# Sums through HBM moved apart, a normalisation moved forward and block products reordered, in a one-core hybrid backbone

## The chip, the core and the metric

The kernel runs on one core of a Trainium2 chip. The metric is device time in microseconds from launch to the last store; smaller is better. TensorE (PE) does the matmuls, VectorE (DVE), ScalarE (ACT) and GpSimd (POOL) the rest, and SyncE (SP) issues most transfers. POOL issues the transfers that add into their destination, ACT a few stores.

## The reference

Two layers on 1024 latent tokens of width 1024, with 256 context tokens, in float32. The change lies in layer 0.

```python
def conformer_conv(va, vg, p):
    u = va * jax.nn.sigmoid(vg)
    u = depthwise_conv(u, p["conv_w"], p["conv_b"], CONV_PAD)   # 31 taps
    return jax.nn.silu(layernorm(u, p["ln_g"], p["ln_b"]))

def rglru_branch(xb, p, h0, with_outputs):
    u = depthwise_conv(xb, p["sconv_w"], p["sconv_b"], SHORT_CONV_PAD)
    u2 = jnp.stack([u, u[:, ::-1]], axis=2)
    a, bx = lru_coeffs(u2, p)            # sigmoid gates, exp, sqrt
    hT, hs = lru_scan(a, bx, h0, with_outputs)
    ...
    y = hs[:, :, 0] + hs[::-1, :, 1]

def even_mixer(h, h0, p):
    z = h @ p["w_in"]
    va, vg, ga, xb, gb = jnp.split(z, ...)
    y_a = conformer_conv(va, vg, p) * jax.nn.silu(ga)
    y_b, hT = rglru_branch(xb, p, h0, True)
    y_b = y_b * jax.nn.silu(gb)
    return jnp.concatenate([y_a, y_b], axis=-1) @ p["w_out"], hT
```

Layer 1 is a pooling mixer with a grouped product (folded into its input weights ahead of time) and an output product; a last RMS norm follows.

## The kernel before

Every array stands transposed: 128 channels on the partitions, 1024 tokens along a row, so a 1024-wide array is eight tiles (`KT = 8`) with two halves of 512 tokens (`HALF`). A float32 factor is split into a high part in the reduced format and the low remainder, and every product is three matmuls: high x high, high x low, low x high. ACT makes the high part (`cast`), DVE or POOL the low one. `mm3_fixed` is one 128-row output half: 8 x 3 matmuls of 512 columns.

Order. The tile framework orders instructions by a simulated timeline, but through most of layer 0 the order is written out by hand: `on(engine, ...)` ties each instruction behind the one before it on its engine, and `act`, `cast`, `gp`, `vec` go through it while `fixed[0]` is true. Each engine runs its list in order, so an instruction that waits holds up all behind it. Where `fixed[0]` is false, the framework places ACT, DVE and POOL instructions; block products of `ga` stay tied on PE. Plain transfers on SP are placed by the framework; those of `sum_copies` are held behind the last weight load (`latest[0]`). `plus` (line 818) is a transfer on POOL's queue that adds its source into its destination, in POOL's written order.

**The rounds (loop over `j`, eight turns; turn `j` is round `j`).** Turn `j` computes `vg`, the recurrence branch input `xb` of the next channel tile, the gates and `va`, makes `u = va * sigmoid(vg)`, and carries the recurrence of the turn before (`state`). On ACT it runs in this order: two tanh (`rec_tanh`, one per direction), the cast of the `va` weights, a sigmoid, the cast `uh`, later exp and sqrt. On DVE `rec_scan` runs once per direction; then `rec_sum` adds the two directions and stores the sum to `yb_raw[j]` in HBM. The tiles rotate: the two tanh of a turn overwrite the backward tile (first) and the forward tile (second) that were scanned at the end of the turn before. `fill(n)` puts n steps of the 31-tap `conv` (one DVE instruction of 512 columns or so) at a place in DVE's order; `conv(j)` turns `us[j]` into its convolution, `ln_sums` adds it up for the norm.

**Sums through HBM.** The product for `ga` is later done by a seven-product block scheme (Strassen-Winograd) on halves of weights, channels and tokens. It needs sums of blocks, and those are made in HBM while the rounds run: `sum_copies(j)` issues the plain copies of turn `j`, `sum_adds(j)` the adding transfers. `h_raw` is the input, high plus low; `neg` two negated halves of it (tiles `n`); `h_ops["t1"]` to `["t4"]` the sums of inputs, `wsums` those of weights.

**After the rounds.** `gb` products, then `wob`: the product of `y_b` with half of the output weights, eight tiles `m` of two halves. `wob_evict` scales a half on ACT, adds `x` on POOL and stores it. Between these, DVE finishes the conv; `mean_parts`, `ln_mean`, `ln_square`, `ln_add`, `ln_root`, `ln_scale`, `ln_silu` are the layer norm of `us`, half by half, with row means by a product with ones (banks `mu` and `ms_ln`; the scale factors `lnr` stay in the banks `c1` and one half of `xb` until `ln_scale` has read them).

**Block products.** For each column `q` (0 to 3) products 1 to 7 of 12 matmuls go into banks `a`, `c`, `b`; `ga_op(n)` splits the n-th weight block in `GORDER`, `ga_raw` loads two of them. After product 1, ACT copies `a` into `b` (line 1645 for q > 0). `ga_silu`, `ga_gate` multiply `us` by the gates, `ga_sum` and `ga_row` make the operands of the next block product, `woa` (the other half of the output). Odd columns use the banks that the norm used. `mods` are DVE dot products of layer 1's modulation, and `wo_steps` the first `woa` weights.

Of the kernel before, what the change touches and what calls it, by code (L numbers as in the profile page):

```python
# [16 lines left out]
S = 1024  # L17
C = 256
# [29 lines left out]
GORDER = ([(0, p) for p in (1, 2, 5, 6, 3, 7)]  # L48
          + [x for q in (1, 2, 3) for x in ((q, 1), (q, 2), (q - 1, 4), (q, 5), (q, 6), (q, 3), (q, 7))] + [(3, 4)])
# [6 lines left out]
def body(ctx, tc, xT, ctxT, cc, ccol, modT, modW, win, gw, wout, wu, grp, wg, wo1, small, edge, ident, outT):  # L56
# [771 lines left out]
    def sum_copies(j):  # L828
        with held(latest[0]):
# [3 lines left out]
            elif j == 1:  # L833
                for n, i in ((0, 0), (1, 1)):
                    nc.sync.dma_start(wsums[n], ga_rows[i][0])
            elif j == 2:
# [6 lines left out]
                nc.sync.dma_start(blocks(h_ops["t3"]), h_rows[:, KH:, HALF[1]])  # L843
            elif j == 3:
                nc.sync.dma_start(wsums[2], wsums[0])
            elif j == 4:
                nc.sync.dma_start(h_ops["t2"], h_ops["t1"])
            elif j == 5:
                nc.sync.dma_start(h_ops["t4"], h_ops["t2"])
                nc.sync.dma_start(wsums[3], wsums[2])  # L850
# [37 lines left out]
    with ExitStack() as actx:  # L888
# [82 lines left out]
        for j in range(KT):  # L971
# [88 lines left out]
            if state is not None:  # L1060
                for d in range(2):
                    rec_scan(state, d)
                rec_sum(state)
# [10 lines left out]
            for n, _ in enumerate(gate_steps(j, (gwh, gwl), (uh, ul), gates)):  # L1074
# [3 lines left out]
                if n == 9:  # L1078
                    w = raw_split(raw, name)
                    rec_input(now, 0)  # L1080
                    if j == 0:
                        sum_adds(j)
            all_of(steps)
            fill(19 if state is None else 6)
# [40 lines left out]
        fill(24)  # L1125
        rec_scan(state, 0)
        raw = raw_load(win[4 * KT + 4], "gb4")
# [6 lines left out]
        rec_sum(state)  # L1134
# [281 lines left out]
    def t_cast(name, q):  # L1416
        hi, lo = ht[name][0][q], ht[name][1][q]
        if name == "t2":
            act(hi, plain(lo), AF.Identity, scale=-1.0)
        else:  # L1420
            cast(hi, plain(lo))
# [11 lines left out]
    wob_ps = {}  # L1433
    for m in range(KT):
        w = gws[KT + m]
        wob_ps[m] = [psum(f"wob{m}_{h}") for h in range(2)]
        steps = [mm3_fixed(wob_ps[m][h], w, (bh, bl), HALF[h]) for h in range(2)]
        for h in range(2):
            for _ in range({0: KT - 1, KT - 1: KH}.get(m, 0)):
                next(steps[h])  # L1440
        if m == KT - 1:
            t_load("t1")
            t_load("t2")
            ga_raw(1)
        for h in range(2):
            all_of(steps[h])
            if (m, h) == (KT - 2, 0):
                while ended[0] < KT:
                    fill(1)
                ln_sums()  # L1450
                for q, parts in enumerate([mean_parts(lnacc[q][:, :H], f"mu{q}") for q in range(2)]):
                    ln_mean(q, parts)
            elif m >= KT - 2:
# [1150 lines left out]
```

## Time and profile before

| what | value |
|---|---|
| runs (3) | median 1310.99 us, 1309.36 to 1311.23 |
| profiled execution | 1312.86 us, its span 1311.1 us |
| granted TensorE clock, mean | 0.98 |
| instructions | 16367 |

The span runs from the first instruction to the last; the profiled execution's time holds what lies around it. Busy time is summed by engine; POOL issues its transfers itself and is held while it does. A row of a timeline has the start and the time in us, the engine, line, operation and output<-inputs, and in brackets the idle time before it and what ended that. A row of the waits names who waited for whom, the sum in us, how often, and the longest. A row of a transfer ends with the median time from issue to landing.

### The profile page before, as it was taken

To read this page: it belongs to the slowest core of one execution; us is meant where nothing else is said; L and a number is where in the kernel's file an instruction comes from. 1 tells how busy PE (TensorE), PEld (TensorE's weight loads), DVE (VectorE), ACT (ScalarE), POOL (GpSimd) and SP (SyncE) were. 2 spreads that over 40 slices of the span, in tenths; PEclk is the share of its full clock that TensorE was granted. 3 is DMA by queue.
4 is the path that set the end of the run, shared out by engine and by line. 5 is a ranking of instruction groups with operands and counts; after the bars stand their busy time and mean duration, and the time that the engine had idled before them with its cause. 6 is when DMAs were issued, how large, how long until landed. Compare 5 with 4: busy or idle time off the path is not lost.

```text
span 1311.1 us, 16367 instructions
## 1 busy us (share of the span) xinstructions
PE 1256.7 (96%) x5818; PEld 1034.1 (79%) x5818; DVE 1158.6 (88%) x1758; ACT 678.4 (52%) x996; POOL 343.8 (26%) x219
## 2 busy tenths in 40 slices
PE   9999989999999999997598999999999999999997
PEld 7788868887888888885476788888888888878786
DVE  7799979998999999988858887999989996977975
ACT  7564666656656433247445445844433443645642
POOL 0015555546454457445441005000000000000002
PEclk9999989999999999998798999999999999999998
DMA  9977835653341224445523656334244324668823
GB/s 371 375 264 230 208 125 137 160 127 115 83 102 57 87 106 153 155 156 203 171 96 120 217 211 216 123 123 157 82 131 150 110 101 137 211 225 314 290 91 128
DMA packets 91873, 216.88 MB, mean 165 GB/s; under 512 B 8784, under 2 KB 24400, under 8 KB 91728
## 3 DMA queue, kind: packets, MB, share of 16 engines
q1 hardware_dynamic: 75840, 194.35, 42.4%
q0 software_dynamic: 4656, 12.58, 5.6%
q10 hardware_dynamic: 11296, 8.92, 2.1%
q8 instruction: 45, 0.74, 0.2%
q14 instruction: 36, 0.29, 0.1%
HBM read 160.24 MB, written 69.21 MB: 175 GB/s over the span
## 4 chain that ended last, share of the span: by engine, by line
PE 54%; DVE 28%; DMA 8%; issue 5%; ACT 3%; POOL 2%; SPq 0%; POOLq 0%; DVEq 0%; ACTq 0%
DVE conv L677 8%; PE wob L677 5%; DVE l L677 5%; PE va L677 3%; PE fold L677 3%; PE xb L677 3%; DVE u L677 2%; PE g L677 2%; DMA modw<-modW 2%; PE vg L677 2%; PE qb_v L1223 1%; PE qb_v L1225 1%; PE qb_ga L677 1%; PE qb_v L1226 1%; PE qb_g L1225 1%
## 5 line engine op out<-in xcount | busy, mean ns | idle before, releaser
L677 DVE SCALAR_TENSOR_TENSOR conv<-u,sm,conv 128x505 f32<-128x505 f32 (+6 forms) x224 | 153.7, 745 | 1.0
L2315 POOL TENSOR_TENSOR o<-x,rr 128x256 f32<-128x256 f32 (+1 forms) x10 | 9.2, 955 | 451.6 <-ACT rr L2315 451.6
L677 ACT ACTIVATE l<-g,sm 128x512 f32<-128x512 f32 (+1 forms) x96 | 58.6, 619 | 57.6 <-PE g L677 56.9
L677 POOL TENSOR_TENSOR l<-l,l 128x1280 f32<-128x1280 f32 x16 | 47.1, 2968 | 30.9 <-ACT l L677 27.4
L677 PE MATMUL va<-h0h,wh_va 128*128 128x512 f32 x128 | 51.0, 398 | 3.6 <-ACT wh_va L677 3.6
L677 PE MATMUL va<-h0h,wl_va 128*128 128x512 f32 x128 | 51.0, 399 | 3.5 <-POOL wl_va L677 3.3
L105 ACT CAST wq_g<-wr_g 128x512 fp32r<-128x512 f32 x48 | 28.2, 621 | 49.7 <-DMA wr_g<-wg 20.4
L677 PE MATMUL gb<-h0h,wl_gb 128*128 128x512 f32 x128 | 49.9, 390 | 1.0 <-POOL wl_gb L677 1.0
L677 PE MATMUL va<-h0l,wh_va 128*128 128x512 f32 x128 | 50.7, 396 | 0.0
L105 ACT CAST wq_v<-wr_v 128x512 fp32r<-128x512 f32 x48 | 28.1, 620 | 42.0 <-DMA wr_v<-wfold 19.2
L677 PE MATMUL gb<-h0h,wh_gb 128*128 128x512 f32 x128 | 49.8, 389 | 0.0
L677 PE MATMUL gb<-h0l,wh_gb 128*128 128x512 f32 x128 | 49.8, 389 | 0.0
L677 PE MATMUL wob<-ybh,wh_wob 128*128 128x512 f32 x128 | 49.8, 389 | 0.0
L677 PE MATMUL wob<-ybl,wh_wob 128*128 128x512 f32 x128 | 49.8, 389 | 0.0
L677 PE MATMUL wob<-ybh,wl_wob 128*128 128x512 f32 x128 | 49.8, 389 | 0.0
L677 DVE TENSOR_TENSOR_SCAN l<-l,l 128x256 f32<-128x256 f32 (+1 forms) x32 | 48.7, 1522 | 1.1
L105 ACT CAST wq_wo<-wr_wo 128x512 fp32r<-128x512 f32 x48 | 28.7, 619 | 39.5 <-DMA wr_wo<-wo 11.9
L677 POOL TENSOR_TENSOR l<-l,uc 128x1280 f32<-128x1280 f32 x16 | 49.0, 3082 | 0.0
L677 DVE SCALAR_TENSOR_TENSOR conv<-cL,wsum,conv 128x506 f32<-128x506 f32 (+3 forms) x70 | 48.1, 744 | 0.2
L677 POOL TENSOR_TENSOR wl_xb<-wr_xb,wh_xb 128x1024 fp32r<-128x1024 f32 x7 | 18.3, 2617 | 104.5 <-ACT wh_xb L677 104.5
L677 PE MATMUL xb<-h0l,wh_xb 128*128 128x512 f32 x112 | 43.8, 391 | 0.0
L677 PE MATMUL xb<-h0h,wh_xb 128*128 128x512 f32 x112 | 43.8, 391 | 0.0
(711 smaller groups left out, 4441.0 us busy)
## 6 DMA issues: line engine op xcount, KB each, us to landing
modw<-modW SPq DMA_DIRECT2D x16, 512.0 KB, 10.2
mod<-modT SPq DMA_DIRECT2D x32, 256.0 KB, 3.0
wr_v<-wfold SPq DMA_DIRECT2D x16, 512.0 KB, 4.3
wr_g<-wg SPq DMA_DIRECT2D x16, 512.0 KB, 4.6
wr_wo<-wo SPq DMA_DIRECT2D x16, 512.0 KB, 4.5
mod<-modT SPq DMA_DIRECT2D x14, 512.0 KB, 4.1
y_b<-y SPq DMA_DIRECT2D x24, 256.0 KB, 3.7
y_t<-y SPq DMA_DIRECT2D x24, 256.0 KB, 3.0
```

The lines of the kernel that those rows point to most:

```text
L105: return (nc.scalar.copy(hi, src), eng.tensor_tensor(out=lo, in0=src, in1=hi.bitcast(F32), op=sub))
L677: last[eng] = f(*args, **kw)
L1223: nc.tensor.matmul(ps, hi, xh[k], start=(first and k == 0), stop=False, skip_group_check=not first)
L1225: nc.tensor.matmul(ps, hi, xl[k], start=False, stop=False, skip_group_check=not first)
L1226: mm = nc.tensor.matmul(ps, lo, xh[k], start=False, stop=(k == KH - 1), skip_group_check=not first)
L2315: tail[eng] = f(*args, **kw)
```

## The change

Six things are done together.

- *Sums apart.* All eight adds into `h_raw` go out in turn 1 (before: four in turn 0, four in turn 1); the loads and copies that use `h_raw` go out in turn 3 (before: turn 2), four copies instead of two, and `t2`, `t4`, `wsums[2]`, `wsums[3]` get their other addend by an add from a finished sum instead of a copy of it. The first copies of `wsums` move from turn 1 to turns 0 and 1.
- *Directions by transfer.* `rec_sum` is gone. After each `rec_scan`, `rec_store` sends that direction to `yb_raw`: the forward one by a plain store on SP, the backward one by an adding transfer on POOL.
- *Fills.* 8 instead of 6 conv steps at the end of turns 1 to 6, and 18 instead of 24 before the last scans.
- *Norm.* The conv has to end, and the means are taken, behind the first half of `wob5` (before: of `wob6`); the squares of the first half follow behind `wob5`'s second (`ln_at(p)`: 10 the means, 11 and 12 the squares of the two halves, 13 the root of the first).
- *Last two output products.* `wob6` and `wob7` each begin with four of eight steps of both halves, then end one after the other, with the roots, scalings, silus and operand casts of the norm and of `t1`, `t2` between their parts in ACT's, DVE's and POOL's order.
- *Block products.* Column 0 joins the loop; the order in a column is 1, 5, (4 of the column before), 2, 6, 3, 7 (before: 1, 2, (4), 5, 6, 3, 7). ACT, DVE and POOL work of column 0 is no longer tied. The weights are split four products ahead, `wo_steps` starts after product 2 of the last column (before: ahead of product 7), and the splits of `t3` and `b22` are no longer held back.

```diff
-GORDER = ([(0, p) for p in (1, 2, 5, 6, 3, 7)]
-          + [x for q in (1, 2, 3) for x in ((q, 1), (q, 2), (q - 1, 4), (q, 5), (q, 6), (q, 3), (q, 7))] + [(3, 4)])
+GORDER = [(q - (p == 4), p) for q in range(4) for p in (1, 5, 4, 2, 6, 3, 7) if q or p != 4] + [(3, 4)]
...
-            elif j == 1:
-                for n, i in ((0, 0), (1, 1)):
-                    nc.sync.dma_start(wsums[n], ga_rows[i][0])
-            elif j == 2:
+            if j < 2:
+                for n in (2 * j, 2 * j + 1):
+                    nc.sync.dma_start(wsums[n], ga_rows[n in (1, 2)][n > 1])
+            if j == 3:
...
-                nc.sync.dma_start(blocks(h_ops["t3"]), h_rows[:, KH:, HALF[1]])
-            elif j == 3:
-                nc.sync.dma_start(wsums[2], wsums[0])
-            elif j == 4:
-                nc.sync.dma_start(h_ops["t2"], h_ops["t1"])
-            elif j == 5:
-                nc.sync.dma_start(h_ops["t4"], h_ops["t2"])
-                nc.sync.dma_start(wsums[3], wsums[2])
+                for n in ("t3", "t2", "t4"):
+                    nc.sync.dma_start(blocks(h_ops[n]), h_rows[:, KH:, HALF[1]])
...
-        if j < 2:
-            for k in range(j * KH, (j + 1) * KH):
+        if j == 1:
+            for k in range(KT):
                 plus(h_raw[:, k * S : (k + 1) * S], plain(hl[k]))
         elif j == 2:
-            for t in neg["12"] + neg["21"]:
-                act(t, t, AF.Identity, scale=-1.0)
             plus(wsums[0], ga_rows[1][0])
             plus(wsums[1], ga_rows[1][1])
         elif j == 3:
-            for n in ("t1", "t3"):
-                for q in range(2):
-                    plus(h_ops[n][:, q * S : (q + 1) * S], neg["12"][q])
+            for t in neg["12"] + neg["21"]:
+                act(t, t, AF.Identity, scale=-1.0)
+            neg_adds("12", ("t1", "t3"))
         elif j == 4:
-            plus(blocks(h_ops["t2"]), h_rows[:, KH:, HALF[1]])
-            plus(wsums[2], ga_rows[1][1])
+            neg_adds("21", ("t4",))
+            plus(wsums[2], wsums[0])
         elif j == 5:
-            for q in range(2):
-                plus(h_ops["t4"][:, q * S : (q + 1) * S], neg["21"][q])
+            plus(h_ops["t2"], h_ops["t1"])
+            plus(h_ops["t4"], h_ops["t1"])
         elif j == 6:
-            plus(wsums[3], ga_rows[0][1])
+            plus(wsums[3], wsums[2])
...
-        def rec_sum(st):
-            hs, hb = st[2][1], st[2][3]
-            vec(nc.vector.tensor_tensor, out=hs[:, C:], in0=hs[:, C:], in1=hb[:, C:], op=add)
-            nc.sync.dma_start(yb_raw[st[0]], hs[:, C:])
+        def rec_store(st, d):
+            latent = st[2][2 * d + 1][:, C:]
+            if d == 0:
+                nc.sync.dma_start(yb_raw[st[0]], latent)
+            else:
+                plus(yb_raw[st[0]], latent)
...
-            fill(19 if state is None else 6)
+            fill(19 if state is None else 6 if final else 8)
...
+    for m in range(KT - 2):
+        wob_begin(m, KT - 1 if m == 0 else 0)
+        for h in range(2):
+            all_of(wob_steps[m][h])
+            ln_at(2 * m + h)
+            wob_evict(m, h)
+            fill(7)
+            ln_sums()
+        gb_weights(KT + m + 2)
+    ga_raw(0)
+    wob_begin(KT - 2, KH)
+    ln_at(12)
+    wob_begin(KT - 1, KH)
+    ln_at(13)
+    t_load("t1")
+    t_load("t2")
+    for h in range(2):
+        all_of(wob_steps[KT - 2][h])
+        wob_evict(KT - 2, h)
+    ga_op(0)
+    ga_op(1)
+    ga_raw(1)
+    ln_root(1, lnparts[1])
+    vec(nc.vector.reciprocal, out=lnr[0], in_=lnrt[0])
+    ln_scale(0)
+    for q in range(2):
+        t_cast("t1", q)
+    t_low("t1", 0, gp)
+    t_low("t1", 1, vtt)
+    for j in range(3):
+        ln_silu(j, 0)
+    all_of(wob_steps[KT - 1][0])
+    wob_evict(KT - 1, 0)
+    vec(nc.vector.reciprocal, out=lnr[1], in_=lnrt[1])
+    for j in range(3, KT):
+        ln_silu(j, 0)
+    for q in range(2):
+        t_cast("t2", q)
+        t_low("t2", q, None)
+    ln_scale(1)
+    all_of(wob_steps[KT - 1][1])
+    wob_evict(KT - 1, 1)
...
+    def ga_run(*args):
+        ga_product(*args)
+        ga_ops(GORDER.index(args[:2]) + 4)
...
-    for q in range(1, KH):
+    for q in range(KH):
...
-            with tc.issue_after(t2_low.ins):
-                split_kept(name)
+            split_kept(name)
```

More of the change, by code (lines that the diff above doesn't have):

```diff
@@ L1124, in body @@
         gb_product(3, gws[3])
-        fill(24)
+        fill(18)
         rec_scan(state, 0)
+        rec_store(state, 0)
         raw = raw_load(win[4 * KT + 4], "gb4")
@@ L1417, in t_cast @@
         hi, lo = ht[name][0][q], ht[name][1][q]
[L1418 to L1421, printed above, removed]
+        kw = dict(scale=-1.0) if name == "t2" else {}
+        (act if fixed[0] else nc.scalar.activation)(hi, plain(lo), AF.Identity, **kw)
     def t_low(name, q, eng):
@@ new lines, in wob_begin, with squares, ln_at @@
+            for _ in range(n):
+                next(wob_steps[m][h])
+    def squares(q):
+        for j in range(KT):
+            ln_square(j, q)
+            if j > 1:
+                ln_add(j - 2, q)
+        for j in (KT - 2, KT - 1):
+            ln_add(j, q)
+    lnparts = {}
+    def ln_at(p):
+        if p == 10:
+            while ended[0] < KT:
+                fill(1)
+            ln_sums()
+            for q, parts in enumerate([mean_parts(lnacc[q][:, :H], f"mu{q}") for q in range(2)]):
+                ln_mean(q, parts)
+        elif p in (11, 12):
+            squares(p - 11)
+            if p == 11:
+                lnparts[0] = mean_parts(lnacc[0][:, :H], "ln0")
+        elif p == 13:
+            ln_root(0, lnparts[0])
+            lnparts[1] = mean_parts(lnacc[1][:, :H], "ln1")
@@ L1636, in ga_ops, with ga_last, run @@
                 ga_op(n)
-    for q in range(1, KH):
+    def ga_run(*args):
+        ga_product(*args)
+        ga_ops(GORDER.index(args[:2]) + 4)
+    def ga_last(q):
+        def run():
+            a, c, b = ga_bank[q]
+            ga_run(q, 4, b, False, True)
+            with tc.high_priority(offset=EVAC):
+                ga_silu(b, 1)
+            ga_gate(q, 1, 0, b)
+        return run
+    for q in range(KH):
         end = q == KH - 1
@@ L1649, in body @@
                 ga_row(i, "t1")
-        ga_product(q, 2, a, False, True)
+        ga_run(q, 5, c, True, True)
+        with tc.high_priority(offset=EVAC):
+            ga_keep(q, "c", c)
+        if q:
+            ga_last(q - 1)()
+        else:
+            for x in range(2):
+                t_cast("t3", x)
+                t_low("t3", x, nc.gpsimd.tensor_tensor)
+        ga_run(q, 2, a, False, True)
+        if end:
+            next(wo_steps)
         with tc.high_priority(offset=EVAC):
             ga_silu(a, 0)
-        ga_last(q - 1)()
         ga_gate(q, 0, 0, a)
         ga_row(q, "b11")
-        if q == 1:
-            ga_row(0, "b11")
-            ga_sum(0, "t1")
-            ga_sum(0, "t3")
         if end:
@@ L1662, in body @@
                 ga_sum(i, "t2")
[L1663 to L1669 removed]
+                ga_row(i, "t2")
+        ga_run(q, 6, b, False, True)
         with tc.high_priority(offset=EVAC):
             ga_keep(q, "b", b)
[L1672 to L1673 removed]
+        if q == 0:
+            for x in range(2):
+                t_cast("t4", x)
+                t_low("t4", x, nc.gpsimd.tensor_tensor)
+        for _ in range((0, 5, 5, 0)[q]):
             next(mods)
[L1675 removed]
+        ga_run(q, 3, c, False, True)
         vtt(out=c, in0=c, in1=ga_part[q, "b"], op=add)
@@ L1684, in body @@
                 ga_row(i, "b21")
-        ga_ops(n + 7)
-        if end:
-            next(wo_steps)
-        ga_product(q, 7, b, False, True)
+        ga_run(q, 7, b, False, True)
         vtt(out=a, in0=b, in1=ga_part[q, "c"], op=add)
```

128 lines of the change are left out of this document (17 added, 111 removed).

## The prediction

> **What bounds the kernel now.** I read the page's engine shares and granted clock first, then busy time by stretch, then the chain of waits, and last the engines' timelines where TensorE stops.
>
> ```profile
> PE 1256.7 (96%) x5818; PEld 1034.1 (79%) x5818; DVE 1158.6 (88%) x1758; ACT 678.4 (52%) x996; POOL 343.8 (26%) x219
> PEclk9999989999999999998798999999999999999998
> ```
>
> TensorE (PE) is busy 96%, VectorE (DVE) 88%. No matmul is removed, so only TensorE's idle time and the time at a lower clock can be won. The next rows give the matmuls' own pace and three stretches of unlike density. Columns: stretch, length, busy time and count of each engine, granted clock, DMA share, GB/s.
>
> ```profile
> 502.84 70.72 PE wob L677 x312
> 580.00:641.00 61.00, 36.81 (x137) 28.06 (x136) 54.65 (x75) 41.46 (x62) 31.29 (x18) 0.78 0.58 191
> 641.00:699.00 58.00, 56.65 (x239) 46.02 (x240) 35.59 (x61) 27.73 (x50) 22.87 (x17) 0.96 0.34 114
> 699.00:720.00 21.00, 15.55 (x55) 11.43 (x54) 20.55 (x35) 12.99 (x24) 0.00 (x0) 0.84 0.36 125
> ```
>
> A 512-column matmul costs 70.72/312 = 0.227 us, a block product of 12 of them 2.72, half an output product (24) 5.44. Count times 0.227, taken from the length, is what is lost: 61 - 31.1 = 29.9 us, 58 - 54.2 = 3.8 and 21 - 12.5 = 8.5. That is 42 us, idle time and half clock together. What TensorE waited for there:
>
> ```profile
> PE qac_ga L677 <- ACT qb_ga L1645: 15.1, 2, 14.4
> PE ms_ln L677 <- ACT mh_ln L677: 4.2, 1, 4.2
> PE qc_woa L1225 <- DVE h0l L106: 3.0, 1, 3.0
> PE va L677 <- ACT wh_va L677: 3.6, 1, 3.6
> ```
>
> The first two are the normalisation: its second mean, and a PSUM bank that it holds until every `us` tile is scaled. The next is an operand of the first `woa` product. The last is in the rounds of the j loop, where TensorE loses time twice:
>
> ```profile
> 165.70:208.20 42.50, 37.66 (x170) 30.86 (x169) 35.09 (x43) 24.60 (x28) 18.58 (x9) 0.92 0.51 130
> 208.20:250.70 42.50, 42.50 (x205) 35.84 (x204) 40.41 (x54) 26.60 (x31) 23.69 (x12) 1.00 0.55 132
> 293.20:337.40 44.20, 42.61 (x205) 35.63 (x204) 39.69 (x50) 26.33 (x30) 22.41 (x10) 1.00 0.48 134
> ```
>
> An undisturbed round does 205 matmuls in 42.5 us. Round 2 lacks 35 of them (42.5 x 35/205 = 7.3 us), round 5 takes 1.7 us more.
>
> **The change part by part: sums through HBM.**
>
> ```profile
> 164.96 1.35 ACT L677 ACTIVATE l<-l,chalf 128x1280 f32<-128x1280 f32 x1
> 175.97 1.36 ACT L677 ACTIVATE l<-l,chalf 128x1280 f32<-128x1280 f32 x1 [9.65 <-DMA yb_raw<-l]
> 215.14 1.36 ACT L677 ACTIVATE l<-l,chalf 128x1280 f32<-128x1280 f32 x1
> 219.69 2.41 POOL L677 TENSOR_TENSOR wl_va<-wr_va,wh_va 128x1024 fp32r<-128x1024 f32 x1
> 224.87 10.88 PE va L677 x48
> SPq L841 <- DMA h_raw<-h0l: 23.0, 2, 18.3
> SPq L850 <- DMA wsum<-win: 8.0, 1, 8.0
> ```
>
> Round 2's loss is the second tanh, which overwrites the forward scan's tile while that is still being stored. The store stood on SP's queue behind loads of `n`, which waited for the sums into `h_raw`. Round 5's is the same with `wsum`. With two rounds between a sum and its use both SP waits go; round 5's 1.7 us is won. Round 3 (the third row and the two below it) shows the slack of an undisturbed round: the low of `va` ends at 222.1, and TensorE's third matmul of `va` wants it at 225.3, 3 us later. In round 3 SP now issues four loads and four copies behind `va3` (6 MB); they run while ScalarE (ACT) and TensorE have their operands, and I cost them at nothing, at most 2 us if round 3's `xb` load is pushed past its cast. The four adds that leave round 0 clear POOL ahead of its `wl` of `va1`: gain 0.5 at most.
>
> **Directions summed by transfer.**
>
> ```profile
> 207.70 1.23 DVE L677 TENSOR_TENSOR l<-l,l 128x1024 f32<-128x1024 f32 x1
> L677 DVE SCALAR_TENSOR_TENSOR conv<-u,sm,conv 128x505 f32<-128x505 f32 (+6 forms) x224 | 153.7, 745 | 1.0
> 150.66 3.52 POOL L677 DMA_DIRECT2D h_raw<-h0l  x4
> h_raw<-h0l POOLq DMA_DIRECT2D x1, 512.0 KB, 5.2
> h_raw<-h0l POOLq DMA_DIRECT2D x1, 512.0 KB, 12.9
> yb_raw<-l SPq DMA_DIRECT2D x1, 512.0 KB, 2.6
> ```
>
> DVE loses eight adds of 1.23 us; six rounds get two more `fill` steps (2 x 0.745 = 1.5), so a round's DVE work grows 0.3 us inside cover that is thin: allow 1 us in all. The conv then stands 12 x 0.745 + 1.23 = about 10 us ahead when the rounds end. In exchange the backward scan's tile is read by an accumulating transfer that waits for the forward store and the second scan. Behind that waiting POOL instruction stand the `wl` of the next `vg` and two products for the tanh; the forward store leaves one scan earlier, so in a clean round POOL is free again before that `wl`. Then the *first* tanh must wait for the accumulate to land. Alone it takes 5.2 us from issue, as the first add in the rows above, against the 7.4 us from the add at 207.70 to the tanh at 215.14: hidden.
>
> Round 2 is different. Round 1 now issues eight adds at 150.66 and the accumulate queues behind them. Of four, the first landed 5.2 after its issue; the fourth 12.9 after its own, which is some 1.7 later: (1.7 + 12.9 - 5.2)/3 = 3.1 us each. The eighth lands at 150.7 + 5.2 + 7 x 3.1 = 178, the accumulate about 181 (at 2.6 each, as the store's row would have it, 177). The first tanh then starts at 177 to 181, the second 1.36 later, at 178 to 182, where it was 175.97: 2 to 6 us later for the `va` cast behind it. I take +4 for round 2, with the bounds -7.3 (no wait at all) and +6.
>
> The Trainium skill, "DMA: Bandwidth & Descriptors", section "Anatomy of one DMA — SWDGE (gpsimd) path", fits such a transfer as 2.0 us plus bytes/436e3, an estimate of 3.2 us for 512 KB and 1.2 more for each behind it. By it the ninth would land near 164 and no tanh would wait. The 3.1 us each of the four adds does not agree.
>
> Rounds together: +4 - 1.7 - 0.5 + 1 = +2.8.
>
> **Norm a product sooner, the last two output products by quarters.** The rows that carry the stretch:
>
> ```profile
> 566.63 1.29 DVE L677 TENSOR_TENSOR lnsum<-lnsum,u 128x512 f32<-128x512 f32 x2
> 574.06 2.48 DVE L677 TENSOR_TENSOR u<-u,mu 128x512 f32<-128x512 f32 x4 [0.23 <-PE mu L677]
> 582.84 0.69 DVE L677 TENSOR_TENSOR lnsum<-mu,lsq 128x512 f32<-128x512 f32 x1
> 573.83 0.69 ACT L677 ACTIVATE wo<-wob,m 128x512 f32<-128x512 f32 x1 [2.95 <-DVE ml_mu L677]
> 584.68 1.13 ACT L677 CAST wq_ga<-wr_ga 128x512 fp32r<-128x512 f32 x2
> 586.16 2.56 POOL L677 TENSOR_TENSOR wq_ga<-wr_ga,wq_ga 128x512 fp32r<-128x512 f32 x2
> 570.30 2.39 POOL L677 TENSOR_TENSOR wl_wob<-wr_wob,wh_wob 128x1024 fp32r<-128x1024 f32 x1
> 574.65 1.31 POOL L677 TENSOR_TENSOR xp<-xp,wo 128x512 f32<-128x512 f32 x1 [1.96 <-issue]
> 608.19 3.35 DVE L677 RECIPROCAL ms_ln<-sq_ln 128x512 f32<-128x512 f32 x1
> 614.38 4.86 DVE L677 TENSOR_TENSOR u<-u,ms_ln 128x512 f32<-128x512 f32 x8
> 602.63 2.01 ACT L677 ACTIVATE h_t2h<-h_t2l 128x1024 fp32r<-128x1024 f32 x2
> 615.09 5.75 ACT L677 ACTIVATE u<-u,sm 128x512 f32<-128x512 f32 x8 [0.82 <-DVE u L677]
> 605.16 1.28 ACT L677 ACT_TABLE_LOAD   x1
> 609.80 2.41 POOL L677 TENSOR_TENSOR h_t3l<-h_t3l,h_t3h 128x1024 fp32r<-128x1024 f32 x1 [0.38 <-ACT h_t3h L677]
> ```
>
> On the old clock (the rounds' +2.8 apart): the mean stands half of `wob5` in, at 502.7 + 5.5 x 10.88 = 562.5. The conv's sums end at 566.63 - 10 + 1.3 = 558, casts and lows two us later: in time. The squares of one half take 574.06 to 583.5 = 9.5 us, so 563.5 to 573; of the other, to 584. Now the order costs something: the cast of `wob7`'s weights stands on ACT behind the first squares and an eviction (to 575.4), its low on POOL behind an `xp` add (1.31) and takes 2.39: 578. TensorE reaches `wob7` at 574.3 and loses 3.3. Then both means find their parts ready, and `wob7` ends at 595.
>
> Next ACT is late. Behind the end of `wob6` (589) it has, in its fixed order, an eviction, two weight casts and a root (0.69, 1.13 and about 0.7), two t1 casts (2.0), the table load (1.28), eight silus (5.75) with an eviction between (0.7), two t2 casts (2.01), another eviction (0.7), and only then the weights of the third block product: 604.5, low at 606. TensorE gets there at 595 + 2 x 2.72 = 600.4: 5 us idle, and one drop of the clock, 1.7. POOL then holds up the rest: seven weight lows (2.56/2 each) and four of t3 and t4 (2.41) are 18.7 us from 604.5, so the ninth product starts its third matmul at 623 and ends near 625.5, with the clock 627. Bounds on this place: 616 if nothing stalls (591.6 + 9 x 2.72), 639 if half the old loss stays. The reciprocals (3.35 each), scalings (4.86 each) and the lows of t1 and t2 between them keep DVE from 586 to some 612 and free the bank before TensorE's copy into it at 619.5. That is where the 14.4 us wait goes.
>
> **Block products reordered.** 18 products are left at 627: 49.0 us, with 2 for single waits 678, where `woa` started at 699.4: **-21.4**. Product 5 between 1 and 2 hides the copy of the bank (0.6); all weights are cast one product earlier; the `woa` weights are loaded after the second product of the last column, so their splits leave the crowded 699 to 720 (DVE 20.55 of 21.00). I take 3 of the 8.5 there, between 0 and 6. The modulation dot products that DVE did in the old gaps lose that cover and slide behind the block products; a later stage could pay up to 3.
>
> Sum: +2.8 - 21.4 - 3 = -21.6. The profiled execution took 1312.86 us with a span of 1311.1; the median of the runs is 1310.99, 1.9 lower. Span after 1289.5, median **1289 us**.
>
> **The rivals.**
>
> (B) Round 2 no longer waits, because the adds run side by side and the accumulate lands 5.2 after its own issue. For it: that landing of the first add. Against: 12.9 for the fourth. Then rounds give -7.3 - 1.7 - 0.5 + 1 = -8.5 in place of +2.8: 1278. By the fit of the skill's DMA page this is what happens.
>
> (C) The new stage keeps half of the old 29.9 us: ACT, DVE and POOL instructions of the first column are no longer in a written order, and one silu or dot product set ahead of the wrong cast repeats part of the 14.4 wait. Old loss 29.9, so some 12 us above my -21.4: 1301. For it: DVE busy 54.65 of 61 there. Against: between 641 and 699 the same scheduler lost only 3.8.
>
> (D) Slower: the accumulate is late in every round. It decides from the place where the wait per round, beyond the 3 us or so of slack found above, passes 24/6 = 4 us: if each lands as the 12.9 row, plus the store ahead of it (2.6), 15.5 from the scan's end against 7.4 + 3 leaves 5 us a round; six rounds make +30, with -24 from the rest +6: 1317. Against: only rounds 1 and 2 have 2 MB of sums just ahead of it; the later ones 0.5 to 2 MB issued over 10 us before.
>
> (E) The accumulates cost as much as the norm gains: (D) with 4 us a round, 6 x 4 - 24 = 0: no change.
>
> **How the numbers follow.** My forecast 0.47, B 0.15, C 0.22, E 0.05, D 0.11. Two runs of this kernel differ by about 0.15%, so 0.2% is what can be told from no change. Faster is the first three, 0.84. The likeliest alone spans 1281 to 1297: half-way from 627 to 616 and to 639, and the 2 us either way of round 2. To leave out no more than 2 in 10 the range takes in C's and most of B's: 1275 to 1305.
>
> **What would show it.** In the trace after: no SP wait at the lines of `h_raw`, `wsum` and `n`; ACT's first tanh of round 2 starting at 177 to 181 behind the `yb_raw` accumulate, with TensorE idle ahead of `va` (7 us or so; none under B); a wait of 2 to 4 us on `wl_wob`, one of 4 to 6 on the third block product's weights; the 14.4 us wait on the bank copy gone, and `woa` starting 17 to 23 us sooner. Wrong if the first tanh waits in rounds 3 to 7 as well, or if TensorE loses over 12 us in the first column.

## The result and the profile after

The change makes the kernel slower: 1324.65 us median (1323.61 to 1326.53), against 1310.17 for the kernel before beside it (1308.81 to 1311.23). The ratio is 1.0113, interval 1.0095 to 1.013. The forecast was 1289. The profiled execution took 1324.78 us with a span of 1323.0, so it stands for the median.

From the page of the kernel after, the engine shares: TensorE is busy 5.4 us longer with the same number of matmuls, but its share of the span is lower.

```profile
PE 1262.1 (95%) x5818; PEld 1037.3 (78%) x5818; DVE 1153.9 (87%) x1749; ACT 678.0 (51%) x996; POOL 352.3 (27%) x229
```

Busy time by stretch, with the columns of the prediction's table: round 2, round 3, and the first block column up to where the second is under way.

```profile
161.60:213.50 51.90, 46.49 (x205) 37.93 (x204) 40.85 (x52) 26.33 (x30) 22.98 (x11) 0.93 0.80 219
213.50:269.00 55.50, 44.91 (x206) 37.29 (x205) 42.56 (x59) 30.24 (x34) 26.53 (x15) 0.91 0.52 118
612.50:659.00 46.50, 33.27 (x118) 25.08 (x118) 41.16 (x53) 28.27 (x43) 30.10 (x17) 0.85 0.69 234
```

Round 3 is the place: 55.5 us for the matmuls that an undisturbed round does in 42.5. Laid out by the starts of TensorE's stages in the two traces (rounded, so that a difference can be off by 0.1):

| stretch | before | after | difference | predicted |
|---|---|---|---|---|
| up to round 2 | 163.7 | 161.6 | -2.1 | -0.5 at most |
| round 2 | 50.2 | 51.9 | +1.8 | +4 |
| round 3 | 42.5 | 55.5 | +13.0 | 0 to 2 |
| rounds 4 to 6 | 129.3 | 132.6 | +3.3 | -1.7 |
| up to the first `wob` | 117.0 | 117.4 | +0.3 | |
| `wob` to `woa` | 196.7 | 191.8 | -4.9 | -21.4 |
| `woa` to the next stage | 145.8 | 146.5 | +0.7 | -3 |
| the rest of the span | 465.9 | 465.7 | -0.2 | 0 to 3 |

What TensorE waits for now (the waits behind the first 60 us: the four largest rows and the one on `wl_wob`). The 14.4 us on the bank copy and the 4.2 on the second mean are gone; a new row stands first.

```profile
PE vg L676 <- POOL wl_vg L676: 17.0, 5, 10.6
PE qb_ga L676 <- DVE qa_ga L730: 4.5, 1, 4.5
PE qa_ga L676 <- ACT qb_ga L1631: 4.5, 1, 4.5
PE qb_ga L676 <- ACT ga_b L1536: 3.6, 2, 2.8
PE wob L676 <- POOL wl_wob L676: 2.1, 1, 2.1
```

**Round 3's loss, link by link.** First the transfers of the kernel after: the four copies of the sums that SP issues between 186.5 and 193 (round 2 is under way, so they stand ahead of the store that round 3 waits for), the forward store issued at 204.97, and the accumulate behind it. The last figure is the median time from issue to landing.

```profile
h_t<-h_raw SPq DMA_DIRECT2D x4, 1024.0 KB, 16.6
yb_raw<-l SPq DMA_DIRECT2D x1, 512.0 KB, 15.9
yb_raw<-l POOLq DMA_DIRECT2D x1, 512.0 KB, 5.0
```

Then POOL's, ScalarE's and TensorE's timelines.

```profile
197.61 2.09 POOL L676 DMA_DIRECT2D wsum<-win  x2
221.39 0.90 POOL L676 DMA_DIRECT2D yb_raw<-l  x1 [21.69 <-DMA yb_raw<-l]
222.00 2.68 POOL L676 TENSOR_TENSOR wl_vg<-wr_vg,wh_vg 128x1024 fp32r<-128x1024 f32 x1
226.47 2.62 ACT L676 ACTIVATE l<-l,chalf 128x1280 f32<-128x1280 f32 x2 [11.54 <-DMA yb_raw<-l]
224.74 0.79 PE L676 MATMUL vg<-h0h,wl_vg 128*128 128x512 f32 x1 [10.59 <-POOL wl_vg L676]
```

The store took 15.9 us; the store at this place in the kernel before took 8.1, and one with nothing ahead of it takes 2.6. POOL stood idle for 21.69 us ahead of its accumulate (10.5 in an undisturbed round of the kernel without adds, below), with the low of `vg`'s weights queued behind it, and TensorE stood 10.59 us for that low. ScalarE waited 11.54 us for the accumulate itself, ahead of the two tanh. Round 2 had the wait that was forecast for it:

```profile
174.60 2.62 ACT L676 ACTIVATE l<-l,chalf 128x1280 f32<-128x1280 f32 x2 [11.61 <-DMA yb_raw<-l]
```

**The first block column.** DVE, POOL and ScalarE in the kernel after, then TensorE's first matmuls of the first, the ninth and the tenth product.

```profile
626.78 0.73 DVE L1563 SCALAR_TENSOR_TENSOR mod<-mod,cH 128x512 f32<-128x512 f32 x1
627.44 2.87 DVE L1563 SCALAR_TENSOR_TENSOR mod<-mod,cH 128x512 f32<-128x512 f32 x1
630.24 2.88 DVE L1563 SCALAR_TENSOR_TENSOR mod<-mod,cH 128x512 f32<-128x512 f32 x1
...
645.79 0.68 DVE L730 TENSOR_TENSOR u<-u,qa_ga 128x512 f32<-128x512 f32 x1
626.90 5.68 POOL L1423 TENSOR_TENSOR h_t3l<-h_t3l,h_t3h 128x1024 fp32r<-128x1024 f32 x2
645.87 0.62 ACT L1396 CAST wq_ga<-wr_ga 128x512 fp32r<-128x512 f32 x1 [10.13 <-DMA wr_ga<-win]
612.55 0.39 PE L676 MATMUL qa_ga<-h0h,wq_ga 128*128 128x512 f32 x1
653.00 0.77 PE L676 MATMUL qb_ga<-h_t4h,wq_ga 128*128 128x512 f32 x1 [4.51 <-DVE qa_ga L730]
657.15 0.39 PE L676 MATMUL qac_ga<-h0h,wq_ga 128*128 128x512 f32 x1
```

With the first column no longer tied, the framework set eleven modulation dot products on DVE (626.78 to 645.79) ahead of the first gate. The gate's operand is ready far sooner: the silu that makes it ends at 634.20. A dot product takes 0.68 us when POOL is quiet and up to 2.88 beside POOL's lows of `t3` and `t4`, which themselves take 5.68 for two. Seven of their loads, which took SP from 627.54 to 642.43, also stood ahead of a weight load (ScalarE idle 10.13 us). Nine products took 657.15 - 612.55 = 44.6 us, where their matmuls need 24.5.

### The profile page after: what moved, and what is told of

The parts are those of the page before. It is cut to its first block, busy times and chain, and to the rows that moved or that the text cites. A ratio compares the mean times of both kernels' runs of the same rounds, so it can differ in the third digit from the quotient of the medians.

```text
span 1323.0 us, 16372 instructions
## 1 busy us (share of the span) xinstructions
PE 1262.1 (95%) x5818; PEld 1037.3 (78%) x5818; DVE 1153.9 (87%) x1749; ACT 678.0 (51%) x996; POOL 352.3 (27%) x229
## 4 chain that ended last, share of the span: by engine, by line
PE 43%; DVE 6%; DMA 2%; issue 2%; ACT 2%; POOL 0%; SPq 0%; POOLq 0%; DVEq 0%; ACTq 0%
PE fold L676 3%; PE qb_v L1220 2%; PE qb_g L1222 2%; PE qb_v L1222 2%; PE qb_g L1223 2%; PE qb_g L1220 2%; PE qb_v L1223 2%; DVE mod L1563 1%; PE qb_ga L676 1%; PE qa_g L1222 1%; PE qc_g L1222 1%; PE qc_g L1220 1%; PE qc_g L1223 1%; PE qa_g L1223 1%; PE qa_g L1220 1%
## 5 line engine op out<-in xcount | busy, mean ns | idle before, releaser
L676 PE MATMUL vg<-h0h,wl_vg 128*128 128x512 f32 x112 | 45.9, 410 | 17.0 <-POOL wl_vg L676 17.0
L676 PE MATMUL wob<-ybh,wl_wob 128*128 128x512 f32 x128 | 50.6, 395 | 2.1 <-POOL wl_wob L676 2.1
L676 PE MATMUL va<-h0h,wh_va 128*128 128x512 f32 x128 | 50.6, 395 | 1.6 <-ACT wh_va L676 1.6
L676 PE MATMUL vg<-h0h,wh_vg 128*128 128x512 f32 x112 | 45.0, 402 | 0.0
L676 PE MATMUL vg<-h0l,wh_vg 128*128 128x512 f32 x112 | 44.8, 400 | 0.0
```

What stands on the lines that cost most here:

```text
L676: last[eng] = f(*args, **kw)
```

## The experiments

Theory A, after the comparison: in the rounds the forward store lands late because sums are on their way, and what waits for it on POOL holds up `vg`; in the block products the dot products that moved ahead hold up the first column. Rivals: the accumulates cost by themselves; the 6 MB of copies cost; the new spacing of the sums costs; the first column is late for POOL's lows or for ScalarE alone.

All ratios are against the kernel before, run beside them.

**Directions on DVE again** (everything else as after):

```diff
                     rec_scan(state, d)
-                    rec_store(state, d)
+                rec_sum(state)
```

> The changed kernel with the two directions added by VectorE again, and one store of the sum behind the second scan (the 8 and 18 fills stay). Theory A (the adding transfer on POOL's queue waits for the forward store, that store lands only when the transfers ahead of it have, and the weight lows of vg stand behind it on POOL): no wait of vg on POOL any more; round 3 falls from 55.5 us to about 43; VectorE's eight adds of 1.23 us cost at most 0.9 us a round, so some 1316 to 1319 us. Theory B (the 6 MB that round 3 issues delay every operand there, whichever way the directions are summed): round 3 stays at 52 us or more, 1325 us or more.

1302.48 us, ratio 0.9936 (0.9915 to 0.9956): faster than both kernels, by more than A forecast. Summing by transfer costs 22 us on the new spacing. (The profiled execution took 1296.96 us, 5.5 less than the median.) Nothing on POOL waits for the store now, but it still lands late behind the copies. The store ahead of round 3 in this kernel, and round 3:

```profile
yb_raw<-l SPq DMA_DIRECT2D x1, 512.0 KB, 12.6
204.20:249.30 45.10, 43.10 (x206) 35.69 (x206) 42.24 (x56) 29.91 (x34) 24.19 (x13) 1.00 0.60 146
```

A store that lands 12.6 us after issue costs a round 2.6 us when no engine but ScalarE, with a tanh, waits for it; in the kernel after, where POOL waits too, 15.9 cost 13.0.

**Old spacing of the sums, directions by transfer** (`sum_copies`, `sum_adds` and the call in turn 0 as in the kernel before):

```diff
-        if j == 1:
-            for k in range(KT):
+        if j < 2:
+            for k in range(j * KH, (j + 1) * KH):
...
                     rec_input(now, 0)
+                    if j == 0:
+                        sum_adds(j)
```

> The changed kernel with the sums through HBM issued as before the change (directions still summed by transfer). Theory A: the forward store now stands on SP behind the loads that wait for the adds into h_raw, so vg waits on POOL in round 2 for 8 us or more, and round 3 is near 44: between 1318 and 1330 us. Theory B: round 3 is near 43 and no other round pays for the transfer, so the rounds are about those of the kernel before: 1308 to 1312 us.

1333.73 us, ratio 1.0179 (1.0143 to 1.0214). Slower than after, beyond both forecasts: the rival that the new spacing costs falls. TensorE's wait for `vg` is larger and SP waits for sums again (waits of that kernel's rounds):

```profile
PE vg L676 <- POOL wl_vg L676: 27.1, 4, 8.1
SPq L840 <- DMA h_raw<-h0l: 22.5, 2, 18.5
```

**Old spacing and directions on DVE, with the new order from the norm on:** both edits above together.

> The changed kernel with both back: sums as before and directions added by VectorE; fills stay at 8 and 18. What is left is the new order from the wob products on. If the stretch from the first wob product to the first woa product is worth by itself what the trace shows (196.7 to 191.9 us, 4.8 us), and VectorE's adds cost up to 0.9 us in six rounds: 1306 to 1311 us. If its gain hangs on the conv being ahead by the saved adds, the mean waits for the conv: 1312 to 1318 us.

1311.61 us, ratio 1.0006 (0.998 to 1.0033). Together with the first two this makes a table of four:

| | directions on DVE | by transfer |
|---|---|---|
| sums as before | 1311.6 | 1333.7 |
| sums two rounds apart | 1302.5 | 1324.7 |

The time lies between the two forecasts. The transfer costs 22 us in both rows, the spacing wins 9 in both columns. That the nines agree is in part chance: by transfer the spacing wins in rounds 4 and 5 (43.4 and 45.2 us against 52.0 and 50.6) and loses in round 3 (55.5 against 51.0), on DVE it wins in each of rounds 2 to 5. And this kernel's rounds are not those of the kernel before: DVE is full. Its round 3, TensorE's wait for it, and DVE and POOL at the start of this round:

```profile
209.40:257.40 48.00, 44.95 (x205) 36.76 (x204) 47.65 (x58) 26.25 (x30) 25.10 (x13) 0.96 0.49 121
PE g L676 <- DVE u L676: 9.5, 5, 3.2
209.91 3.51 DVE L676 TENSOR_TENSOR cL<-u 128x512 f32<-128x512 f32 x1
209.92 6.32 POOL L676 TENSOR_TENSOR l<-l,uc 128x1280 f32<-128x1280 f32 x2
```

The add and eight conv steps alone do not fill it: 58 DVE instructions take 47.65 us here and 42.05 in round 4 of the kernel with the directions on DVE. Most of the difference is two instructions that ran beside POOL's here: `cL<-u` took 3.51 us (0.69 there) and the one ahead of it, `edge_junk`, 2.37 (0.16).

**The order from the norm on, alone:** the same with the old six and 24 conv steps.

```diff
-            fill(19 if state is None else 6 if final else 8)
+            fill(19 if state is None else 6)
...
-        fill(18)
+        fill(24)
```

> The order of the norm, the output products and the block products alone: sums through HBM and rounds as in the kernel before, directions summed on DVE, and its numbers of conv steps (6 in a round, 24 at the end). Theory: with 8 conv steps and the add DVE was full in the old rounds (47.65 us busy of 48.00) and they took 9 us more; with 6 they are the old ones again, and the new order alone gives its 5 us less what the later conv takes off: 1303 to 1309. Rival: the norm a product sooner hangs on the freed conv, and without it the output products wait 10 us for the mean: 1310 to 1316.

1309.28 us, ratio 1.0001 (0.9984 to 1.0017): nothing is won or lost, where the theory had up to 6 us. The conv is late and the mean waits for it, and `wob` to `woa` takes what it took before (196.7); the profiled execution is the slowest of this kernel's runs, 7 us above their median, so only this stretch and the wait are read:

```profile
505.10:701.60 196.50, 172.88 (x718) 138.62 (x717) 165.72 (x240) 92.25 (x144) 96.69 (x61) 0.94 0.45 153
PE mu L676 <- ACT mh_mu L676: 5.4, 1, 5.4
```

So the new order alone is worth nothing: it needs the conv ended sooner. With eight conv steps a round and the add on DVE the same stretch took 189.5 us with the old spacing and 191.1 with the sums apart. The old spacing paid for the steps in rounds 2 to 5 (190.4 us against 172.8), so the room for the conv came from the spacing, not from taking the add away.

**The sums' adds behind the accumulate** (directions by transfer, spacing as after; only the place of the adds in POOL's order moves):

```diff
                     rec_scaled(state, d)
-                sum_adds(j)
...
                     rec_store(state, d)
+                sum_adds(j)
```

> The changed kernel with each round's adding transfers into the HBM sums issued behind the two stores of the directions instead of ahead of them; nothing else. Theory A: the forward store lands some 3 us after issue where no copies are on SP, so the vg waits of rounds 1 to 6 go, except round 3 (there the store stands behind 6 MB of copies on SP's own queue): 6 to 9 us less than the changed kernel, 1316 to 1319 us, and the first tanh of round 2 starts with its operand. Rival (the adding transfer itself is what is slow, wherever it stands): no change, 1323 to 1326 us.

1308.23 us, ratio 0.9986 (0.9971 to 1.0002): 16 us less than after, twice what A forecast. Stores with only adds issued *behind* them land as if alone; the one that round 3 waits for still comes behind the copies. The stores that rounds 2, 3, 4 and 5 wait for (the last took 3.7 with no adds at all, below), then the accumulate of round 4:

```profile
yb_raw<-l SPq DMA_DIRECT2D x1, 512.0 KB, 2.6
yb_raw<-l SPq DMA_DIRECT2D x1, 512.0 KB, 8.1
yb_raw<-l SPq DMA_DIRECT2D x1, 512.0 KB, 2.6
yb_raw<-l SPq DMA_DIRECT2D x1, 512.0 KB, 3.9
yb_raw<-l POOLq DMA_DIRECT2D x1, 512.0 KB, 5.3
```

What is left is in rounds 2 and 3 (48.3 and 47.8 us): there TensorE waits 3.9 and 3.4 us for the low of `vg`, which POOL now begins behind the issuing of the adds (eight of them keep it 7.42 us).

**No adds of sums at all** (the sums lack their second operand; copies and accumulates of directions stay):

```diff
     def sum_adds(j):
+        if j != 3:
+            return
...
             for t in neg["12"] + neg["21"]:
                 act(t, t, AF.Identity, scale=-1.0)
-            neg_adds("12", ("t1", "t3"))
```

> The changed kernel without its adding transfers of the sums through HBM: the plain copies stay (6 MB in round 3), the directions are still summed by transfer, and the sums lack their second operand. Theory A: POOL's accumulate waits for the forward store, and the store lands late because adding transfers are in flight. Without them stores land some 3 us after issue but in round 3, where the copies still run; rounds 2 and 4 to 6 come to 42.5 to 44 us and round 3 to at most 48: 1297 to 1306. Rival B: the accumulate itself is what costs, whatever else is on the way; the rounds keep 1 to 3 us each and round 2 stays near 50: 1312 to 1325. Rival C: the 6 MB of copies cost the most; round 3 stays at 52 to 55, the others at 42.5: 1307 to 1312.

1296.71 us, ratio 0.9892 (0.9862 to 0.9921): A's number, 0.3 us under its range; the rival that the accumulate itself costs falls, and so does the one that the copies cost the most. The store that round 2 waits for, the one that round 3 waits for (behind the 6 MB of loads and copies), and rounds 2 and 3:

```profile
yb_raw<-l SPq DMA_DIRECT2D x1, 512.0 KB, 2.6
yb_raw<-l SPq DMA_DIRECT2D x1, 512.0 KB, 7.6
161.60:204.10 42.50, 42.50 (x206) 35.85 (x205) 40.68 (x53) 26.47 (x30) 19.18 (x10) 1.00 0.58 205
204.10:248.30 44.20, 42.81 (x206) 35.80 (x205) 42.22 (x57) 30.14 (x34) 23.01 (x11) 1.00 0.30 77
```

An undisturbed round is 42.5 us with the accumulate, as it is with the add on DVE: TensorE's matmuls fill it in both, so taking eight adds off DVE wins nothing there.

**Copies of `t2` and `t4` a round later** (directions by transfer):

```diff
-                for n in ("t3", "t2", "t4"):
-                    nc.sync.dma_start(blocks(h_ops[n]), h_rows[:, KH:, HALF[1]])
+                nc.sync.dma_start(blocks(h_ops["t3"]), h_rows[:, KH:, HALF[1]])
+            if j == 4:
+                for n in ("t2", "t4"):
+                    nc.sync.dma_start(blocks(h_ops[n]), h_rows[:, KH:, HALF[1]])
```

> The changed kernel with the copies of t2 and t4 (2 MB of reads and as much of writes) in round 4 in place of round 3. Theory A: in round 3 the store is held by the copies and by the adds into wsum together, so half of round 3's 13 us goes and round 4 takes some of it on: 1315 to 1321. Rival C (the bulk of the copies is all of round 3's loss): round 3 near 45, 1309 to 1314. Rival: only adds hold a store, copies don't: no change, 1322 to 1327.

1314.21 us (1307.2 to 1320.7), ratio 1.0034 (1.0012 to 1.0055), at the edge between A's range and that of C. Round 3 in its trace:

```profile
213.20:257.80 44.60, 42.80 (x206) 35.77 (x205) 42.34 (x57) 30.25 (x34) 24.93 (x14) 1.00 0.64 159
```

Some 11 of round 3's 13 us are gone with 2 MB of copies moved and the adds into `wsum` still ahead of the store; some 11 were gone too with all the copies there and no adds (44.2 us). So neither makes the loss alone: it takes both. The runs scatter by 13 us and the profiled one is the fastest, so no closer split is read from it.

**The dot products held** (from here on with the directions on DVE):

```diff
+                    with held(mod_after[0]), held(latest[0] if mod_after[0] is not None else None):
                         nc.sync.dma_start(raw, modT[1, n, :, HALF[q]])
                         nc.vector.scalar_tensor_tensor(out=raw, in0=raw, scalar=1.0, in1=cH, op0=mult, op1=mult,
                                                        accum_out=m1p[:, n, q : q + 1])
...
-        ga_gate(q, 1, 1, a)
+        mod_after[0] = ga_gate(q, 1, 1, a)
```

> The changed kernel with the directions summed on DVE (1302.5 when it was timed), and the modulation dot products that the scheduler had set ahead of the first column's gates written behind that column's last gate, their loads behind the weight loads. Theory: they held DVE, the loads and POOL's lows in the first column (5.1 and 2.9 us of waits and the lower clock behind them); the ninth block product ends some 8 us sooner: 1291 to 1296. Rival: the dot products only move into the second column and hold that up, or the column waits for POOL's lows as before: 1300 to 1305.

1294.45 us, ratio 0.9876 (0.9844 to 0.9909): 8 us less than with the directions on DVE alone, as the theory had it. POOL's two lows of `t3` and DVE's first gate in that kernel, and the first matmuls of the first and of the tenth product:

```profile
601.41 4.77 POOL L1420 TENSOR_TENSOR h_t3l<-h_t3l,h_t3h 128x1024 fp32r<-128x1024 f32 x2
608.74 0.69 DVE L730 TENSOR_TENSOR u<-u,qa_ga 128x512 f32<-128x512 f32 x1 [7.37 <-ACT qa_ga L1537]
587.06 0.39 PE L676 MATMUL qa_ga<-h0h,wq_ga 128*128 128x512 f32 x1
621.71 0.39 PE L676 MATMUL qac_ga<-h0h,wq_ga 128*128 128x512 f32 x1
```

Nine products in 34.7 us, not 44.6, and the gate waits for its operand, not for DVE. POOL's two lows are back at 4.77. Part of the gain is lost again: against the directions on DVE alone the ninth product ends 11.7 us sooner, the first `woa` product starts 6.2 sooner (184.9 us after the output products' start, not 191.1). The largest wait left is in the last column, where dot products now stand, near to what the rival had (waits of that kernel):

```profile
PE qb_ga L676 <- ACT ga_b L1533: 6.8, 2, 5.6
```

**Casts of the third and fourth weights sooner** (directions on DVE, dot products as after):

```diff
     wob_evict(KT - 1, 0)
+    ga_op(2)
+    ga_op(3)
...
-    ga_cast(2)
-    ga_low(2)
-    ga_cast(3)
-    ga_low(3)
```

> The changed kernel with the directions summed on DVE, and the casts and lows of the third and fourth block products' weights right behind the first eviction of the last output product, ahead of five silus, the t2 casts and the second eviction. Theory: the third block product's 4.4 us wait goes, 3 to 5 us: 1297.5 to 1299.5. Rival: the silus and t2 operands are later by as much and the next wait takes its place: 1301 to 1304.

1297.37 us, ratio 0.99 (0.9868 to 0.9931), an interval that overlaps that of the directions on DVE alone. The number fits the theory, its reason does not: the wait that should have gone is still there.

```profile
PE qb_ga L676 <- DVE qa_ga L730: 8.2, 1, 8.2
PE qa_ga L676 <- ACT qb_ga L1626: 4.5, 1, 4.5
```

The third product waits for ScalarE's copy of bank `a`, which stands behind silus and casts; and the wait for DVE grew from 5.1 us to 8.2. That this edit by itself gains is not shown.

**Combined**, with ScalarE's order of the first column written out (bank copy first, then the `t2` casts, silus last):

```diff
+        fixed[0] = q == 0
         ga_run(q, 1, a, True, True)
-            nc.scalar.copy(b, a)
+            (cast if fixed[0] else nc.scalar.copy)(b, a)
...
                 t_cast("t4", x)
                 t_low("t4", x, nc.gpsimd.tensor_tensor)
+            fixed[0] = False
+            for j, h in ([(0, 1), (KH, 0), (KH, 1), (3, 0)] + [(j, 0) for j in range(KH + 1, KT)]
+                         + [(j, 1) for j in late_silu[2:]]):
+                with held(last["act"]):
```

> The changed kernel with the directions summed on DVE, the dot products held, the casts of the third and fourth weights sooner, and ScalarE's order of the first column written out: the bank copy right behind the first block product, then the t2 casts, the other copies and casts, and thirteen silus last. Theory: what was left in the first column (4.5 us at the third product for the bank copy, 4 to 7 us at the seventh and ninth) stood behind silus on ScalarE; the ninth product ends near +120 us after the output products' start in place of 128.5: 1285 to 1290. Rival: the silus now hold up the gates or the next column's casts, and the loss moves one column on: 1292 to 1296.

1296.04 us, ratio 0.988 (0.9866 to 0.9895): the rival. The wait for the bank copy falls to 1.2 us, but waits at the fourth product (`t2` lows, 3.6 us) and at the ninth (3.1) take its place, and the ninth product ends 129.1 us after the output products' start, much as with the dot products held alone (128.3). This other order of ScalarE's work moved the wait and did not shorten it; whether another would is not shown.

**With the copies of `t2` and `t4` a round later:** 

> The same with the copies of t2 and t4 in round 4 in place of round 3. Theory: with the sum on DVE the store of round 3 lands 12.6 us after issue behind the copies and costs that round 2.6 us (45.1 against 42.5); with 2 MB less there it lands in time and round 4 has the room: 1 to 3 us less than the kernel before it in this list. Rival: round 4 pays the same, since the adds into the same operands wait for the copies: within 1 us of it.

1291.09 us, ratio 0.9848 (0.9829 to 0.9866): the theory's way and more than its 1 to 3 us (4.9 by the medians, 3.3 of it in round 3). Round 3 in the kernel ahead of it in this list, then in this one:

```profile
204.10:249.90 45.80, 43.10 (x205) 35.69 (x205) 42.35 (x56) 29.91 (x34) 24.19 (x13) 1.00 0.59 145
204.00:246.50 42.50, 42.50 (x205) 35.84 (x204) 42.18 (x57) 30.31 (x34) 23.69 (x13) 1.00 0.64 166
```

**With four dot products out of the last column:**

```diff
-        for _ in range((0, 5, 5, 0)[q]):
+        for _ in range((0, 5, 3, 0)[q]):
...
-        for _ in range((0, 4, 2, 0)[m // 2]):
+        for _ in range((0, 5, 3, 0)[m // 2]):
```

> The best kernel so far (1291.1) with four of the modulation dot products of the second half moved from the last block column into the output products behind it. Theory: they stood on DVE ahead of the last column's sums, and with them a copy on ScalarE was late by 5.7 us: that wait and its drop of the clock go, 1284 to 1288. Rival: the copy is late for DVE's sums themselves or for the splits of the next weights: 1290 to 1292.

1285.73 us, ratio 0.9828 (0.9797 to 0.9858): 24 us less than before, the best version. The wait for the copy `ga_b` is 1.4 us where it was 5.7; `wob` to `woa` takes 180.0 us, 16.7 less than before.

```profile
PE qb_ga L676 <- ACT ga_b L1532: 1.4, 1, 1.4
```

## Why the prediction was wrong, step by step

**What held.** All SP waits on `h_raw` and `wsum` went. The first tanh of round 2 was forecast at 177 to 181 and came at 174.60, because the eight adds began at 144.81, not at 150.66; from the first add's issue to the accumulate's landing it was 29.7 us, as forecast (26 to 30). Counted from the round's start the `va` cast behind it came 1.9 us later than in the kernel before, and round 2 lost +1.8 against +4; TensorE stood 3.3 us at `va` (and 2.1 at `vg`), not 7. In the norm, the waits of 14.4 and 4.2 us went, the mean stood 59.8 us after the output products' start (59.8 forecast), the waits at `wob7` were 2.1 and 0.4 against 3.3, and the block products began 93.6 us after that start (92.2).

**What was named as a sign of being wrong.** Both signs came. The first tanh waited for the accumulate in rounds 3 to 6 as well (11.54, 1.72, 3.47 and 2.16 us), and TensorE lost 20 us in the first column (44.6 us for 24.5 us of matmuls).

**Failed step 1: "in a clean round POOL is free again before that `wl`" and "6 MB ... I cost them at nothing, at most 2".** The first sentence is true (42.5 us in the clean rounds of the kernel without adds); the mistake is that hardly a round is clean. The prediction took 2.6 us for the store from a row without other transfers, and used it in every round. The same trace of the kernel before had other rows too: in the four rounds with adds and a copy on the way its stores took 9.5, 8.1, 7.1 and 7.1 us, and only ScalarE's tanh waited for them. Two of these, issued at 208.96 and at 251.13:

```profile
yb_raw<-l SPq DMA_DIRECT2D x1, 512.0 KB, 8.1
yb_raw<-l SPq DMA_DIRECT2D x1, 512.0 KB, 7.1
```

The case against rival (D), that later adds are issued over 10 us before, did not carry over: the forward store leaves a scan earlier, which the prediction counted as a gain, and so it went out 4 to 6 us behind the adds ahead of rounds 4 to 6 (252.24 to 258.05 in the first of them). Nor did the 6 MB run in round 3: SP issued them from 186.84 on, in round 2 and ahead of the store at 204.97. In the kernel after, the stores that rounds 3 to 6 wait for showed 15.9, 8.3, 10.1 and 8.8 us from issue to landing, the accumulate on POOL waited for each, and what was queued behind it on POOL was the low that TensorE needs next. The terms: round 3 +13.0 in place of 0 to 2, rounds 4 to 6 +3.3 in place of -1.7. This was rival (D), a late accumulate, with the place right and the mechanism half right: (D) had the accumulate slow, 12.9 us; the accumulates took 5.0, and the store ahead of them was slow. By the runs: transfers issued *ahead* of the store hold it (2.6 us without adds, 2.6 with the adds issued behind it, up to 15.9 behind copies and adds that are still on the way).

The Trainium skill, "DMA: Bandwidth & Descriptors", section "Queues, rings and completion order", says that the write that signals a transfer's end lands only after every earlier write from the same DMA engine, across its queues. By it a store can be held by adds on another queue, and the trace agrees so far: 15.9 us where 6 MB of loads and copies and two adds had been issued before, 2.6 where none had. It does not mean that a store waits for all that was issued ahead of it: the store of 150.66 landed at 160.5, the last of the eight adds issued ahead of it at 172.2. Whether this rule or the sharing of the DMA engines makes the delay, no run here tells apart. The prediction should have weighed it; it speaks against this change.

**Failed step 2: the first block column, -21.4.** The ninth product ends 138.2 us after the output products' start, where the working had 627 - 502.7 = 124.3 and 136 at its upper bound. Of the 13.9 us, 10 to 12 are the dot products (138.2 here and 140.0 with the directions on DVE against 128.3 with them held). The prediction named them ("lose that cover and slide behind the block products; a later stage could pay up to 3") and had them slide the wrong way: untied, they were set *ahead* of the gates, because their operands were ready. The other 2.6 us of this term lie between the ninth product and `woa` (53.6 us against 51). This was rival (C), priced at 12 us against the 16.5 measured. Its case against, that the same scheduler lost only 3.8 us between 641 and 699, came from a stretch where the first column's order had been written by hand up to its end.

That a dot product takes 2.88 us beside POOL's lows, and a pair of lows 5.68 in place of 4.77, is contention of these two engines. The Trainium skill, "SBUF — State Buffer", section "SBUF: two separate sides", has DVE work with two inputs in SBUF and POOL's lock each other out of a shared port for a whole instruction. The times agree: 2.88 is 0.68 and most of one low of 2.4 (half of 4.77).

**A smaller miss.** The wait at the third product was forecast at 5 us for its weights. It was 4.5 for the bank copy, and 0.5 more for the weights' low behind that: ScalarE was late, as forecast, but with the copy as well, which the prediction had hidden behind product 5. The right size is in part luck, and the experiment that moved the weights alone did not remove the wait.

**Where the sum stands.** Up to `wob` +16.3 (+2.8 forecast), `wob` to `woa` -4.9 (-21.4), behind it +0.5 (-3): the span grew by 11.9 us, forecast -21.6.

## What to carry to other kernels

Price a transfer by what has been issued ahead of it, on any queue, and then ask which engine stands waiting for its landing and what is queued behind on that engine: a late store cost a round 2.6 us when one tanh waited for it (12.6 us from issue to landing) and 13.0 when POOL did (15.9). When an order written by hand is given back to a scheduler, list every instruction whose operands are ready early and that the old order held off; those move forward, not back. An engine that is busy 88% need not be the bottleneck: with the sums apart, taking eight adds off DVE gained nothing in a clean round, while spacing the sums and holding the dot products back gained 9 and 8 us. But look at when its instructions run: DVE was full in the old spacing with eight conv steps, since two of them stood beside POOL's.

## What the runs showed of the hardware that was not expected

- A plain store to HBM of 512 KB lands 2.6 us after issue alone (3.7 in one round of the kernel without adds), and up to 15.9 us after issue with other transfers into HBM on the way, issued ahead of it on SP's or POOL's queue. Adds issued behind it leave it at 2.6 to 3.9. It need not wait for all that is ahead: one landed 11.7 us before an add that had been issued before it.
- An accumulate of 512 KB into HBM takes 4.9 to 5.4 us alone in the rounds, and 5.3 to 5.6 with one to eight more issued right behind it. Eight adds in a train with the accumulate as the ninth were done 29.7 us after the first was issued.
- A DVE product of two SBUF operands (0.68 us) takes up to 2.88 beside POOL's subtractions of 1024 columns, and a pair of these 5.68 in place of 4.77. A DVE sum of 512 columns (0.69) took 3.51 beside POOL's work on 1280.
